# Copying queries and keys into block order on POOL for the two dilated patterns of a hybrid gMLP and attention block

## Chip, cores and metric

The kernel runs on one core of one Trainium2 chip. The metric is the device time of one execution in microseconds (us). Every time below is from that core. The engines are named as in the profile: PE multiplies matrices, PEld loads its stationary operand, DVE, ACT and POOL work element by element, and SP issues nearly all transfers.

## What is computed

One layer on 2048 tokens of width 1024: an input product with a 1024 x 9216 matrix, a gated spatial mixing branch (a), a dilated attention branch (b), gates, two projections and a final norm. The part that the change touches is the attention, with 16 heads of width 64 and three patterns (window, dilation) = (128, 1), (512, 4), (2048, 16). Each pattern takes the tokens by stride and attends within blocks of 128:

```python
def to_blocks(t):
    t = t.reshape(Bn, H, L, dilation, Dh).transpose(0, 1, 3, 2, 4)
    ...
    return t.reshape(Bn, H, dilation, nb, BLOCK, Dh)

qb, kb, vb = to_blocks(q), to_blocks(k), to_blocks(v)
kw, vw = with_prev(kb), with_prev(vb)      # the block before and this one
...
s = jnp.einsum('bhrnqd,bhrnkd->bhrnqk', qb, kw) * (Dh ** -0.5)
s = s - slopes[...] * (dist * dilation)
s = jnp.where(valid, s, NEG_INF)
m = jnp.max(s, axis=-1); p = jnp.exp(s - m[..., None]); l = jnp.sum(p, axis=-1)
o = jnp.einsum('bhrnqk,bhrnkd->bhrnqd', p, vw) / l[..., None]
```

The three results of a head are mixed by their softmax denominators.

## The kernel before

**Stages.** First come normalised inputs and the q, k, v, gate and branch-a products (up to about 1430 us of the profile). Then comes `window`, the attention of all 16 heads, which is interleaved with the remaining dense products, called *fill* (80 products of 24 matmuls each, L116). Last comes `final` (from about 2430 us): the projection of b, the output product and the norm.

**Numbers.** Dense products are exact sums of three products of high and low parts, so every weight block of 1024 x 128 is split on POOL inside the window: `whi` (L85) and then `wlo` (L86). Queries and keys are float16. `Q` holds a head's high and low parts of the queries on its 128 partitions, `KH` and `KL` the high and the low keys, twice each; all three are [128, 2048], tokens in their natural order along the row.

**Attention.** A head has three patterns, taken in the order p = 2 (dilation 16), p = 1 (dilation 4), p = 0 (dilation 1). A pattern has 16 blocks of 128 queries in four groups g. A group goes through three stages, each one step or more behind the other:

- `stage_s`: scores. Per block two matmuls, L407 with `KH` and L408 with `KL`, both with the block's queries of `Q` as the stationary operand, into `ss` in PSUM (two buffers). DVE adds the bias `B` and takes the row maximum (L414, into `S` and `m4`), and L417 scales the four maxima into column 65 of the output tile (`ob` or `OC`). ACT takes the exponential (L422).
- `stage_t`, two steps later: transposes of `S` on PE (L439) into `pt`, then the high part `ph` on ACT (L442) and the low part `pl` on DVE (L443).
- `stage_o`, three steps after the scores: L456 to L458 multiply by `V`, ACT copies the result out (L459).

p = 2 blocks have one block of keys (128 columns). In p = 1 every fourth block has one and the others two (256 columns); in p = 0 only the first has one. Which columns a block reads is said by `cols`:

```python
if p == 0:
    return t[:, P * b:P * (b + n)]
if p == 1:
    return t.rearrange("p (a q) -> p q a", q=4)[:, b // 4, P * (b % 4):P * (b % 4 + n)]
return t.rearrange("p (a q) -> p q a", q=16)[:, b]
```

so that p = 1 reads every 4th float16 (8 bytes apart) and p = 2 every 16th (32 bytes apart).

**Combine.** When p = 0 of a head is done, `combine` runs in pieces during the second half of the next head's p = 2 and its p = 1: small DVE operations (L478 to L488), then four times L497 on DVE (scaling `OC`), L499 on POOL (adding) and L502 on DVE (adding into `cb`). After every second head come four transposes (L509) and L513.

**What sets the order.** PE's order is the program's, since each piece is queued behind the one before (`seg`). The other engines' and SP's queues are filled by a scheduler that takes instructions by priority and by when it reckons them ready; each queue then runs strictly in its order. Tiles that share a tag share its buffers, and an instruction that writes a tile waits until all readers of the buffer's last tile are done.

Of the kernel before, what the change touches and what calls it, by code (L numbers as in the profile page):

```python
# [16 lines left out]
P = 128  # L17
# [10 lines left out]
class Prog:  # L28
# [6 lines left out]
    # ---------------------------------------------------------------- setup  # L35
    def setup(self):
# [15 lines left out]
        # largest |g_norm|, and the scales of q, k (pair of heads) and v (four heads)  # L52
# [21 lines left out]
    # -------------------------------------------------------------- helpers  # L74
# [13 lines left out]
    def wblock(self, wp, w, c0, width, scale=None):  # L88
        """columns c0..c0+width of a weight, as exact high and low parts;
        scale: [P, 1] that gets a scale under which no product with h leaves float16"""  # L90
# [6 lines left out]
        if scale is not None:  # L97
            # |h @ w| <= |h| |w column| <= (32 max|g|) (32 max|w|)
# [40 lines left out]
    # ------------------------------------------------------- normalised input  # L139
# [4 lines left out]
    def split_X(self, X, k, src):  # L144
        """src fp32 -> X[k] exact high and low parts"""
# [29 lines left out]
    def load_X(self, qd, src):  # L175
        X = self.alloc_X(qd % 2)
        for k in range(KC):
            t = self.wk.tile([P, 512], F32, name="xl", tag="xl")
# [15 lines left out]
    def unit_rows(self, wp, X, hf, w, c0, evac, scale=None):  # L194
        """128 tokens on partitions, 256 columns at a time, two such in a bank"""
# [16 lines left out]
    # ---------------------------------------------------------------- q and k  # L212
    def ev_qk(self, dst, s):
        nc = self.nc

        def ev(nb, qd, ps):
            hi = self.wk.tile([P, 512], F16, name="qh", tag="qh")
            lo = self.wk.tile([P, 512], F16, name="ql", tag="ql")
# [36 lines left out]
    # --------------------------------------------------------------- branch a  # L255
# [66 lines left out]
    # ------------------------------------------------------------- gates of b  # L322
# [24 lines left out]
    # -------------------------------------------------------------- attention  # L347
# [28 lines left out]
    def cols(self, t, p, b, n):  # L376
        """n = 1: columns of block b; n = 2: of block b and the next one"""
        if p == 0:
            return t[:, P * b:P * (b + n)]
        if p == 1:  # L380
            return t.rearrange("p (a q) -> p q a", q=4)[:, b // 4, P * (b % 4):P * (b % 4 + n)]
        return t.rearrange("p (a q) -> p q a", q=16)[:, b]

    def stage_s(self, at, G):
        nc = self.nc
        h, p, g = G["h"], G["p"], G["g"]
        Q, KH, KL, B = G["qk"]
# [7 lines left out]
        S = at.tile([P, 4, 256], F32, name="S", tag="S", bufs=4)  # L395
# [3 lines left out]
        for i2 in range(2):  # L399
            ps = self.ps.tile([P, 2, 256], F32, name="ss", tag="ss", bufs=2)  # L400
            for i in range(2):
# [3 lines left out]
                q = self.cols(Q, p, b, 1)  # L405
                w0 = b - 1 if prev else b
                nc.tensor.matmul(ps[:, i, :n], q, self.cols(KH, p, w0, n // P), start=True, stop=False)  # L407
                self.pe = nc.tensor.matmul(ps[:, i, :n], q, self.cols(KL, p, w0, n // P), start=False, stop=True)  # L408
# [360 lines left out]
```

## Time and profile before

| | |
|---|---|
| median of 3 runs | 2826.39 us (2821.72 to 2830.69) |
| span of the profiled execution | 2821.4 us |
| PE busy | 2724.5 us, 97% of the span |
| DVE / ACT / POOL busy | 1195.5 / 1063.8 / 625.6 us |
| first score matmul, last score matmul | 1467.7 us, 2413.8 us |
| score matmuls L407 + L408, busy | 258.5 + 264.7 us (768 each) |

The profiled execution shows no time outside its span; the fastest of the three runs is 0.3 us above the span and their median 5.0 us. Busy time of PE is summed over overlapping matmuls, so what one matmul costs is read from the distance between the starts of consecutive ones, not from its duration. A head starts every 60 us or so.

### The profile page before, as it was taken

The page shows a single profiled execution, that of the slowest core. Times are in us where ns is not written, and L with a number is a line of the kernel's source. Part 1 is how long each engine was busy: PE and PEld are TensorE (multiplying, and loading weights), DVE is VectorE, ACT ScalarE, POOL GpSimd, SP SyncE. Part 2 cuts the span into 40 slices and gives each one's busy share as a digit, 9 for nine tenths or more (in the row PEclk, how much of TensorE's full clock was granted, in tenths as well). Part 3 has the DMA queues.
Part 4 walks back from the last instruction along what each step waited for, and adds up shares of the span by engine and source line. Part 5 has one row for each costly group of instructions (what it writes and reads, how often), then busy time and mean ns, then how long its engine had stood idle before and what let it go on. Part 6 is the DMA issues. An engine that isn't in the chain of part 4 may idle for free.

```text
span 2821.4 us, 44790 instructions
## 1 busy us (share of the span) xinstructions
PE 2724.5 (97%) x17504; PEld 2273.2 (81%) x17504; DVE 1195.5 (42%) x3186; ACT 1063.8 (38%) x2039; POOL 625.6 (22%) x398
## 2 busy tenths in 40 slices
PE   6899899999999999999999999999999999899998
PEld 4779897888887889988877777777777777678887
DVE  6232104331003111013336666677677777555443
ACT  4312212122123222221126666666666666333221
POOL 2322211223233221212231221233333333100000
PEclk9999999999999999999999999999999999999999
DMA  7633402224345333202254556656677676665442
GB/s 230 177 101 85 93 16 76 67 87 134 101 136 155 93 102 84 66 28 68 67 163 115 153 149 169 166 169 182 186 213 221 192 208 187 205 208 183 153 151 74
DMA packets 489332, 381.68 MB, mean 135 GB/s; under 512 B 152224, under 2 KB 414752, under 8 KB 489120
## 3 DMA queue, kind: packets, MB, share of 16 engines
q1 hardware_dynamic: 488688, 378.75, 46.4%
q8 instruction: 137, 2.24, 0.3%
q14 instruction: 75, 0.61, 0.1%
q10 hardware_dynamic: 432, 0.07, 0.0%
HBM read 277.42 MB, written 101.32 MB: 134 GB/s over the span
## 4 chain that ended last, share of the span: by engine, by line
PE 84%; DMA 3%; DVE 3%; ACT 2%; issue 2%; POOL 1%; SPq 0%; DVEq 0%; ACTq 0%; POOLq 0%
PE pj L116 65%; PE ss L407 5%; PE ss L408 5%; PE pt L439 4%; PE po L456 1%; PE po L458 1%; PE po L457 1%; DMA wraw<-in_w_proj_b 1%; PE pt L297 1%; DMA v_d<-vst 1%; ACT junk L281 1%; DVE X L148 1%; PE pt L509 0%; POOL wlo L86 0%; DMA xl<-ya_d 0%
## 5 line engine op out<-in xcount | busy, mean ns | idle before, releaser
L116 PE MATMUL pj<-X,whi 128*128 128x512 f32 x4608 | 1472.0, 398 | 21.4 <-ACT whi L83 8.3
L116 PEld LDWEIGHTS pj<-X,whi 128*128 128x128 f32 x4608 | 868.2, 190 | 202.6 <-ACT whi L83 10.3
L116 PE MATMUL pj<-X,wlo 128*128 128x512 f32 x2304 | 915.5, 397 | 16.1 <-POOL wlo L86 10.8
L86 POOL TENSOR_TENSOR wlo<-wraw,whi 128x1024 fp32r<-128x1024 f32 (+1 forms) x176 | 458.5, 2606 | 763.7 <-ACT whi L83 688.3
L116 PEld LDWEIGHTS pj<-X,wlo 128*128 128x128 f32 x2304 | 437.9, 190 | 109.8 <-POOL wlo L86 12.7
L116 PE MATMUL pj<-whi,X 128*128 128x256 f32 x2048 | 360.7, 279 | 6.9 <-DVE vst L238 6.7
L83 ACT CAST whi<-wraw 128x1024 fp32r<-128x1024 f32 (+1 forms) x152 | 173.2, 1140 | 505.2 <-PE pj L116 445.7
L116 PEld LDWEIGHTS pj<-whi,X 128*128 128x128 f32 x2048 | 312.9, 188 | 8.2 <-issue 7.2
L414 DVE CUSTOM_DVE_ANT_0 S<-ss,B 128x256 f32<-128x256 f32 (+1 forms) x768 | 244.6, 361 | 143.7 <-PE ss L408 142.6
L116 PE MATMUL pj<-wlo,X 128*128 128x256 f32 x1024 | 285.6, 279 | 2.7 <-POOL vst L233 2.7
L422 ACT ACTIVATE S<-S,ob,iqk 128x128 f32<-128x128 f32 (+1 forms) x512 | 231.8, 525 | 95.4 <-DVE ob L417 95.3
L407 PE MATMUL ss<-KH,Q 128*128 128x256 f16 (+1 forms) x768 | 258.5, 356 | 6.9 <-DVE m L414 6.8
L408 PE MATMUL ss<-KL,Q 128*128 128x256 f16 (+1 forms) x768 | 264.7, 358 | 0.0
L443 DVE SCALAR_TENSOR_TENSOR pl<-pt,ph 128x512 f16<-128x512 f32 x320 | 203.4, 653 | 89.8 <-ACT ph L442 88.1
L442 ACT ACTIVATE ph<-pt 128x512 f16<-128x512 f32 x320 | 167.5, 560 | 119.6 <-PE pt L439 119.5
L116 PEld LDWEIGHTS pj<-wlo,X 128*128 128x128 f32 x1024 | 192.6, 188 | 2.9 <-POOL vst L233 2.9
L85 POOL TENSOR_SCALAR whi<-wraw 128x1024 fp32r<-128x1024 f32 x64 | 69.3, 1083 | 539.0 <-PE pj L116 508.6
L116 PE MATMUL pj<-WO,X 128*128 128x512 f32 x768 | 180.1, 395 | 0.9 <-ACT X L632 0.8
L116 PEld LDWEIGHTS pj<-WO,X 128*128 128x128 f32 x768 | 144.1, 188 | 36.2 <-ACT X L632 1.2
L439 PEld LDWEIGHTS pt<-ident,S 128*128 128x128 f32 x1200 | 146.1, 144 | 28.9 <-DVE pl L443 3.6
L439 PE MATMUL pt<-ident,S 128*128 128x128 f32 x1200 | 165.6, 275 | 2.7 <-DVE pl L443 2.7
L422 ACT ACTIVATE S<-S,OC,iqk 128x256 f32<-128x256 f32 (+1 forms) x256 | 131.8, 584 | 52.5 <-DVE OC L417 52.5
(105 smaller groups left out, 2422.5 us busy)
## 6 DMA issues: line engine op xcount, KB each, us to landing
wraw<-in_w_in SPq DMA_DIRECT2D x136, 512.0 KB, 4.1
V<-v_d SPq DMA_DIRECT2D x48, 520.0 KB, 4.2
o_d<-ob SPq DMA_DIRECT2D x32, 528.0 KB, 4.3
OC<-o_d SPq DMA_DIRECT2D x32, 528.0 KB, 5.2
wraw<-in_w_in SPq DMA_DIRECT2D x16, 1024.0 KB, 5.6
wraw<-in_w_proj_a SPq DMA_DIRECT2D x32, 512.0 KB, 5.3
wraw<-in_w_proj_b SPq DMA_DIRECT2D x32, 512.0 KB, 4.5
v_d<-vst SPq DMA_DIRECT2D x128, 65.0 KB, 3.5
```

The source lines that it names most:

```text
L83: nc.scalar.copy(hi, raw)
L85: nc.gpsimd.tensor_scalar(out=hi, in0=raw, scalar1=1.0, scalar2=0.0, op0=ALU.mult, op1=ALU.add)
L86: self.w_lo.tensor_tensor(out=lo, in0=raw, in1=hi.bitcast(F32), op=ALU.subtract)
L116: self.pe = nc.tensor.matmul(out, st(a, k), mv(b, k), start=first and n == 0, stop=last and n == len(todo) - 1)
L148: self.x_lo.tensor_tensor(out=X[k][1], in0=src, in1=X[k][0].bitcast(F32), op=ALU.subtract)
L407: nc.tensor.matmul(ps[:, i, :n], q, self.cols(KH, p, w0, n // P), start=True, stop=False)
L408: self.pe = nc.tensor.matmul(ps[:, i, :n], q, self.cols(KL, p, w0, n // P), start=False, stop=True)
L414: nc.vector.tensor_tensor_reduce(out=S[:, j, :n], in0=ps[:, i, :n], in1=B[:, bo:bo + n], scale=1.0, scalar=-3e38, op0=ALU.add, op1=ALU.max ...
L422: nc.scalar.activation(S[:, i, :rng[i]], S[:, i, :rng[i]], AF.Exp, bias=ob[:, i, 65:66], scale=self.iqk[:, pr:pr + 1])
L439: self.pe = nc.tensor.transpose(px[:, j * P:(j + 1) * P], G["S"][:, i, c * P:(c + 1) * P], self.ident)
L442: nc.scalar.activation(ph[:, :n], px[:, :n], AF.Copy, scale=PSCALE)
L443: nc.vector.scalar_tensor_tensor(out=pl[:, :n], in0=px[:, :n], scalar=PSCALE, in1=ph[:, :n], op0=ALU.mult, op1=ALU.subtract)
```

## The change

`permute` is new: for each head and for p = 2 and p = 1, POOL copies `Q`, `KH` and `KL` into `perm_` tiles in which every block's 128 columns lie next to each other. That is 6 copies of [128, 2048] float16 a head, 96 in all; p = 0 still reads the raw tiles. The scores then read plain slices. The copies for p = 1 of a head are written out after the scores of groups 0, 1 and 2 of its p = 2, and those for p = 2 of the next head after the same groups of p = 0. They use three tags with two buffers each.

Room is made by fewer buffers: `V` 2 for 4, `S` 3 for 4, `ph` and `pl` 3 for 4, and one tag `ld` with 3 buffers in place of `xl` (2) and `gal` (2, used for `gal` and `sbg`). The staging tiles `qh` and `ql` move to a pool of their own that is gone by the time of the window. The load of the next pattern's `V` is written out at group 3 of a pattern and no longer at group 0. Comments are dropped; the PE order is the same, with `perm_` tiles in place of the raw ones.

```diff
-            t = self.wk.tile([P, 512], F32, name="xl", tag="xl")
+            t = self.wk.tile([P, 512], F32, name="xl", tag="ld", bufs=3)
...
-        g = self.wk.tile([P, 512], F32, name="gal", tag="gal")
+        g = self.wk.tile([P, 512], F32, name="gal", tag="ld", bufs=3)
...
-        V = at.tile([P, 16, 130], F16, name="V", tag="V", bufs=4)
+        V = at.tile([P, 16, 130], F16, name="V", tag="V", bufs=2)
...
-    def cols(self, t, p, b, n):
...
+    def permute(self, at, t, p):
+
+        r = at.tile([P, T], F16, name=f"perm_{t.name[:2]}", tag=f"perm{len(self.perm_tags) % 3}", bufs=2)
+        self.perm_tags.append(0)
         if p == 1:
...
+            self.nc.gpsimd.tensor_copy(r.rearrange("p (q n a) -> p q n a", q=4, n=4),
+                                       t.rearrange("p (n a q) -> p q n a", q=4, n=4))
+        else:
+            self.nc.gpsimd.tensor_copy(r.rearrange("p (q a) -> p q a", q=16),
+                                       t.rearrange("p (a q) -> p q a", q=16))
+        return r
...
-        S = at.tile([P, 4, 256], F32, name="S", tag="S", bufs=4)
+        S = at.tile([P, 4, 256], F32, name="S", tag="S", bufs=3)
...
-                q = self.cols(Q, p, b, 1)
-                w0 = b - 1 if prev else b
-                nc.tensor.matmul(ps[:, i, :n], q, self.cols(KH, p, w0, n // P), start=True, stop=False)
-                self.pe = nc.tensor.matmul(ps[:, i, :n], q, self.cols(KL, p, w0, n // P), start=False, stop=True)
+                q = Q[:, P * b:P * b + P]
+                w = slice(P * (b + 1) - n, P * (b + 1))
+                nc.tensor.matmul(ps[:, i, :n], q, KH[:, w], start=True, stop=False)
+                self.pe = nc.tensor.matmul(ps[:, i, :n], q, KL[:, w], start=False, stop=True)
...
-            ph = at.tile([P, 512], F16, name="ph", tag="ph", bufs=4)
-            pl = at.tile([P, 512], F16, name="pl", tag="pl", bufs=4)
+            ph = at.tile([P, 512], F16, name="ph", tag="ph", bufs=3)
+            pl = at.tile([P, 512], F16, name="pl", tag="pl", bufs=3)
...
-        qk[0] = self.load_qk(at, 0)
+        raw = {0: self.load_qk(at, 0)}
+        qk[0, 2] = [self.permute(at, t, 2) for t in raw[0][:3]]
...
+                if g == 3 and j + 1 < n:
+                    q = j // 4 + 1
+                    vt[q // 3, 2 - q % 3] = self.load_v(at, q // 3, 2 - q % 3)
                 if g == 0:
-                    q = j // 4 + 1
-                    if q < 3 * NH:
-                        h2, p2 = q // 3, 2 - q % 3
-                        vt[h2, p2] = self.load_v(at, h2, p2)
...
+                G.update(qk=qk[h, p] if p else raw[h][:3], B=raw[h][3], V=vt[h, p], OC=OC, O=O)
                 run(self.stage_s(at, G))
+
+                nxt = {2: (h, 1), 0: (h + 1, 2)}.get(p)
+                if nxt and nxt[0] < NH and g < 3:
+                    qk.setdefault(nxt, []).append(self.permute(at, raw[nxt[0]][g], nxt[1]))
```

**POOL's queue, around p = 1 of a head in the later half.** The names: `B` is the next head's bias, `OC` the four additions of the combine, `whi` and `wlo` the halves of a fill weight block. Before:

```order
L359 TENSOR_SCALAR B<-B,sqk 128x640
L499 TENSOR_TENSOR OC<-OC 128x4x64 x3
L85 TENSOR_SCALAR whi<-wraw 128x1024
L86 TENSOR_TENSOR wlo<-wraw,whi 128x1024
L499 TENSOR_TENSOR OC<-OC 128x4x64
L85 TENSOR_SCALAR whi<-wraw 128x1024
L86 TENSOR_TENSOR wlo<-wraw,whi 128x1024
```

And now, where L384 is a copy for p = 2 of the next head, L381 one for its p = 1, and L504 the addition that was L499:

```order
L384 COPY perm_KH<-KH 128x2048
L359 TENSOR_SCALAR B<-B,sqk 128x640
L384 COPY perm_Q__19353<-Q 128x2048
L504 TENSOR_TENSOR OC<-OC 128x4x64
L384 COPY perm_KL<-KL 128x2048
L85 TENSOR_SCALAR whi<-wraw 128x1024
L86 TENSOR_TENSOR wlo<-wraw,whi 128x1024
L504 TENSOR_TENSOR OC<-OC 128x4x64 x3
L85 TENSOR_SCALAR whi<-wraw 128x1024
L86 TENSOR_TENSOR wlo<-wraw,whi 128x1024
L381 COPY perm_Q__19667<-Q 128x2048
L381 COPY perm_KH<-KH 128x2048
```

The three copies for p = 2 stand ahead of and among the additions of the combine, and the three for p = 1 follow at once, behind the weight blocks.

**DVE's queue, two groups of p = 0.** `S,m` are the row maxima of L414, `pl` the low part of the transposed probabilities, of which a group has two. Before:

```order
L443 SCALAR_TENSOR_TENSOR pl<-pt,ph 128x512
L417 TENSOR_SCALAR OC<-m_12134,niqk 128x4
L443 SCALAR_TENSOR_TENSOR pl<-pt,ph 128x384
L414 ISA S,m_12205<-ss,B 128x256
L414 ISA m_12205 128x1
L414 ISA S,m_12205<-ss,B 128x256
L414 ISA m_12205 128x1
```

And now, with L448, L422 and L419 for L443, L417 and L414:

```order
L448 SCALAR_TENSOR_TENSOR pl<-pt,ph 128x512
L422 TENSOR_SCALAR OC<-m_12164,niqk 128x4
L419 ISA S,m_12239<-ss,B 128x256
L419 ISA m_12239 128x1
L419 ISA S,m_12239<-ss,B 128x256
L419 ISA m_12239 128x1
L448 SCALAR_TENSOR_TENSOR pl<-pt,ph 128x384
```

The second `pl` of a group, whose buffer is now that of the group before, has moved behind the first half of the next scores.

More of the change, by code (lines that the diff above doesn't have):

```diff
@@ L216, in ev @@
         def ev(nb, qd, ps):
-            hi = self.wk.tile([P, 512], F16, name="qh", tag="qh")
-            lo = self.wk.tile([P, 512], F16, name="ql", tag="ql")
+            hi = self.wq.tile([P, 512], F16, name="qh", tag="qh")
+            lo = self.wq.tile([P, 512], F16, name="ql", tag="ql")
             sc = s[:, nb:nb + 1]
@@ L386, in stage_s @@
         h, p, g = G["h"], G["p"], G["g"]
-        Q, KH, KL, B = G["qk"]
+        Q, KH, KL = G["qk"]
+        B = G["B"]
         period = (16, 4, 1)[p]
@@ L509, in combine @@
                 self.pe = nc.tensor.transpose(px[:, r * P:(r + 1) * P], cb[:, 4 * g + r], self.ident)
-            sb = self.wk.tile([P, 512], F32, name="sbg", tag="gal")
+            sb = self.wk.tile([P, 512], F32, name="sbg", tag="ld", bufs=3)
             nc.sync.dma_start(out=sb, in_=self.bg_d[g][i * P:(i + 1) * P])
@@ L525, in window @@
         qk, vt = {}, {}
+        self.perm_tags = []
         att_total = (0.109 * 2 + 0.088) * 75 * NH + 8 * 4 * 0.45
@@ L558, in window @@
                     if p == 1 and h + 1 < NH:
-                        qk[h + 1] = self.load_qk(at, h + 1)
+                        raw[h + 1] = self.load_qk(at, h + 1)
                 if g == 0:
                     O = OC[:, 0] if p == 0 else at.tile([P, 16, 66], F32, name="ob", tag="ob", bufs=2)
-                G.update(qk=qk[h], V=vt[h, p], OC=OC, O=O)
+                G.update(qk=qk[h, p] if p else raw[h][:3], B=raw[h][3], V=vt[h, p], OC=OC, O=O)
                 run(self.stage_s(at, G))
+                nxt = {2: (h, 1), 0: (h + 1, 2)}.get(p)
+                if nxt and nxt[0] < NH and g < 3:
+                    qk.setdefault(nxt, []).append(self.permute(at, raw[nxt[0]][g], nxt[1]))
             if 2 <= j < n + 2:
@@ L663, in load_Y @@
         for k in ks:
-            t = self.wk.tile([P, 512], F32, name="xl", tag="xl")
+            t = self.wk.tile([P, 512], F32, name="xl", tag="ld", bufs=3)
             self.nc.sync.dma_start(out=t, in_=self.yb_d[qd][k * P:(k + 1) * P])
@@ L679, in run @@
             hp = s1.enter_context(tc.tile_pool(name="hp", bufs=2))
+            self.wq = s1.enter_context(tc.tile_pool(name="wq", bufs=2))
             X = [None, None]
```

4 lines of the change are left out of this document (removed).

## Prediction

> **What bounds the kernel now.** I read the page's busy shares first, then the window of the attention by stretches, then the single matmuls in the timeline, then who waited for whom.
>
> ```profile
> PE 2724.5 (97%) x17504; PEld 2273.2 (81%) x17504; DVE 1195.5 (42%) x3186; ACT 1063.8 (38%) x2039; POOL 625.6 (22%) x398
> ```
>
> PE looks like the bound, but its busy time is modelled. The timeline's starts say more. Columns: start, duration, engine, line, operation. First p = 2 (128 columns, 32 bytes apart), then p = 1 (128 and 256 columns, 8 bytes apart), then p = 0 (dense):
>
> ```profile
> 1700.89 0.42 PE L407 MATMUL ss<-KH,Q 128*128 128x128 f16 x1
> ...
> 1702.56 0.41 PE L408 MATMUL ss<-KL,Q 128*128 128x128 f16 x1
> ...
> 1715.81 0.28 PE L407 MATMUL ss<-KH,Q 128*128 128x128 f16 x1
> ...
> 1716.03 0.41 PE L407 MATMUL ss<-KH,Q 128*128 128x256 f16 x1
> ...
> 1717.18 0.41 PE L408 MATMUL ss<-KL,Q 128*128 128x256 f16 x1
> ...
> 1733.85 0.22 PE L407 MATMUL ss<-KH,Q 128*128 128x128 f16 x1
> ...
> 1733.96 0.27 PE L407 MATMUL ss<-KH,Q 128*128 128x256 f16 x1
> ...
> 1740.17 0.28 PE L407 MATMUL ss<-KH,Q 128*128 128x256 f16 x1
> ...
> 1740.94 0.27 PE L408 MATMUL ss<-KL,Q 128*128 128x256 f16 x1
> ```
>
> Distance over count: p = 2, 1.67 us over 7 steps, 0.239 us a matmul; p = 1, 0.22 over 2 = 0.110 (128 columns) and 1.15 over 5 = 0.230 (256); p = 0, 0.11 over 2 = 0.055 (128) and 0.77 over 7 = 0.110 (256). The same shapes cost 4.3 and 2.1 times the dense price when their columns lie apart.
>
> Now the stretches of one early and one late head, each cut at the first scores of p = 2, p = 1 and p = 0. Columns: stretch, length, busy us of PE, PEld, DVE, ACT and POOL, granted clock, DMA share, GB/s.
>
> ```profile
> 1519.60:1540.00 20.40, 20.40 (x179) 16.09 (x176) 10.87 (x52) 11.74 (x31) 4.23 (x3) 1.00 0.77 201
> 1540.00:1558.10 18.10, 18.10 (x150) 13.60 (x147) 16.22 (x53) 11.14 (x26) 6.52 (x6) 1.00 0.15 46
> 1558.10:1576.50 18.40, 18.40 (x189) 15.70 (x186) 11.68 (x45) 14.44 (x32) 0.58 (x1) 1.00 0.59 157
> ...
> 1934.50:1954.80 20.30, 20.30 (x177) 15.98 (x174) 9.92 (x51) 12.79 (x32) 6.98 (x5) 1.00 0.73 180
> 1954.80:1972.80 18.00, 18.00 (x148) 13.36 (x145) 16.91 (x51) 11.95 (x28) 7.73 (x6) 1.00 0.57 176
> 1972.80:1995.00 22.20, 22.20 (x215) 19.07 (x212) 13.67 (x48) 14.15 (x31) 6.89 (x4) 1.00 0.67 191
> ```
>
> PE is full in all three and the clock is 1.00. But in p = 1, where the combine runs, DVE is busy 16.2 to 16.9 of 18 us: PE bounds it by little. In p = 2 and p = 0 DVE has room. PE's own waits over the window are small, and all but one group name DVE:
>
> ```profile
> PE ss L407 <- DVE m L414: 6.8, 6, 2.4
> PE po L456 <- ACT ob L459: 3.1, 3, 1.1
> PE pt L439 <- DVE pl L443: 2.7, 2, 2.5
> PE po L458 <- DVE pl L443: 1.3, 1, 1.3
> ```
>
> Where the longest comes from matters most for this change. Rows of POOL, DVE and PE around 2155 us:
>
> ```profile
> 2151.38 2.39 POOL L86 TENSOR_TENSOR wlo<-wraw,whi 128x1024 fp32r<-128x1024 f32 x1
> ...
> 2152.15 1.64 DVE L417 TENSOR_SCALAR ob<-m,niqk 128x4 f32<-128x4 f32 x1
> ...
> 2158.40 0.22 PE L407 MATMUL ss<-KH,Q 128*128 128x128 f16 x1 [2.36 <-DVE m L414]
> ```
>
> L417 writes four numbers a partition. Here it takes 1.64 us and ends at 2153.79, 0.02 us after POOL's L86 (2153.77). The same pairing stands at 1919.96:
>
> ```profile
> 1919.58 2.69 POOL L86 TENSOR_TENSOR wlo<-wraw,whi 128x1024 fp32r<-128x1024 f32 x1
> ...
> 1919.96 2.35 DVE L417 TENSOR_SCALAR OC<-m,niqk 128x4 f32<-128x4 f32 x1
> ...
> 1925.68 0.55 PE L439 MATMUL pt<-ident,S 128*128 128x128 f32 x3 [2.47 <-DVE pl L443]
> ```
>
> Undisturbed, L417 takes 0.22 us (next rows). So some DVE operations stand still until POOL's running instruction ends, and PE then waits 2.4 us. Operations that read PSUM do not; L148 (0.68 us alone, 1.53 beside an L85), the combine's L483 to L502 and L417 do.
>
> ```profile
> 1918.50 1.53 DVE L148 TENSOR_TENSOR X<-xl,X 128x512 fp32r<-128x512 f32 x1 [0.67 <-ACT X L147]
> ...
> 1998.81 0.22 DVE L417 TENSOR_SCALAR ob<-m,niqk 128x4 f32<-128x4 f32 x1
> 1998.94 0.69 DVE L443 SCALAR_TENSOR_TENSOR pl<-pt,ph 128x512 f16<-128x512 f32 x1
> ...
> 2033.98 0.68 DVE L148 TENSOR_TENSOR X<-xl,X 128x512 fp32r<-128x512 f32 x1
> ```
>
> **The change part by part.**
>
> *Dense scores, PE.* Per head, p = 2 has 32 matmuls of 128 columns: 32 x (0.239 - 0.055) = 5.9 us. p = 1 has 24 of 256 and 8 of 128: 24 x (0.230 - 0.110) + 8 x (0.110 - 0.055) = 3.3 us. That is 9.2 us a head, 147 us for 16. PE's order is unchanged, so this is on the path as long as the others keep up: p = 2 would go from 20.3 to 14.4 us, p = 1 from 18.0 to 14.7.
>
> *The copies, POOL.* No copy of this kind stands in the trace. The nearest rows have one operand and are dense:
>
> ```profile
> L85 POOL TENSOR_SCALAR whi<-wraw 128x1024 fp32r<-128x1024 f32 x56 | 60.9, 1087 | 492.8 <-PE pj L116 473.8 <-DVE pl L443 16.5 <-DMA wraw<-in_w_proj_a 2.4
> ...
> L499 POOL TENSOR_TENSOR OC<-OC 128x256 f32<-128x256 f32 x60 | 49.0, 821 | 115.7 <-DVE ob L417 32.7 <-DVE OC L497 29.5 <-ACT ph L442 23.1
> L359 POOL TENSOR_SCALAR B<-B,sqk 128x640 f32<-128x640 f32 x14 | 12.1, 863 | 51.4 <-DMA B<-in_bias 51.4
> ```
>
> 2048 elements at L85's rate are 2.1 us, the lower bound for both kinds. Upper bounds scale it by what PE pays for the stride: 2.1 x 2.1 = 4.4 us (p = 1) and 2.1 x 4.3 = 9.1 us (p = 2). For the value I take PE's cost per strided column as the rate at which such columns come out of memory: 0.230/256 = 0.90 ns (8 bytes), below POOL's own 1.06 ns, so p = 1 stays at 2.1 us; 0.239/128 = 1.87 ns (32 bytes), 2048 of them 3.8 us, with a start 4.0 us for p = 2. A head's POOL work in the late part is then five weight blocks at 1.09 + 2.4, four L499, one L359 and 3 x (2.1 + 4.0): about 40 us of 55 to 60. POOL is not the bound by sum.
>
> *The copies' effect on DVE.* The p = 2 copies write buffers that the last p = 2 scores of the head before free, so they run at the end of p = 2 and in p = 1, where DVE is fullest. I walk that stretch by hand, t = 0 at that release, first p = 1 scores due at 3.6. `KH` copy 0 to 4.0: DVE does two L414 and stands in L483 from 0.4 (3.6 us lost). L359 4.0 to 4.8; `Q` copy to 8.8: DVE gets through L484 and stands in L485 (3.7 lost). The third waits for L499, which waits for L497, so it runs about 11.6 to 15.6 and holds L417 for some 2 us. Together 9.3 us. p = 1 then needs 16.6 of DVE (mean of the two heads) + 9.3; one group, 3.7 us, can be carried into p = 0, since `ss` has two buffers. 22.2 us instead of 18.0. In p = 0 the three 2.1 us copies cost about 1.4 each (DVE has one 0.69 us L443 or so to do before it stands), with the 3.7 carried 13.7 + 4.2 + 3.7 = 21.6 of 22.2 late, 19.6 of 18.4 early: +0.5 on the mean. p = 2 keeps its 14.4, DVE at 10 to 12.
>
> *The sum.* 15 heads x (-5.9 + 4.2 + 0.5) = -18; the last head makes no copies for a next one, -9.2. Together -27 from 2821.4: 2794, and with the median 5 above the profiled span, 2799 us.
>
> *Fewer buffers.* `S` with 3: L414 of group j reuses the buffer whose transposes (group j-3) PE has done just ahead of these scores; nothing. `ph`/`pl` with 3: the second pair waits until L456 to L458 of the group before have read; it is used a group, 4 us, later, and DVE's queue has L414 moved ahead of it, so the cover is that group; without it, the 0.7 us of one `pl` a group. `V` with 2: the load waits on SP for L458 of two patterns ago, now right behind, and is needed four groups (17 us) later against 4.2 us to landing; what is queued behind it (`wraw`, `o_d`) waits under a group:
>
> ```profile
> V<-v_d SPq DMA_DIRECT2D x48, 520.0 KB, 4.2
> ```
>
> `ld`: `gal`, `sbg` and `xl` share three buffers; a transfer of 5 us against 12 us a product; `xl` in the last phase gets one more. I cost all at 0 to 5 us and take 0.
>
> *Start.* The first scores need three copies (12 us) after their loads; six products of fill, 144 matmuls, stand ahead. 0, at worst 5.
>
> **The rivals.**
>
> *Cheap copies.* POOL may not mind the stride: 2.1 us for all. Each copy in p = 1 then blocks 1.9 us less: 45 x 1.9 = 86 more, 2713 us. For it: POOL's rate is half of PE's per column. Against: 32 bytes cost PE fourfold.
>
> *A half surcharge.* POOL may pay a fixed part for the stride; midway between 2.1 and 4.0 the p = 2 copy is 3.1 us, 45 x 0.9 = 40 more, 2759 us. [...] No row here shows a strided POOL read.
>
> *Slower.* Every further us of the p = 2 copy stands in DVE's way in p = 1, 45 us in all. The gain is gone at 4.0 + 27/45 = 4.6 us; at 5.5 us the kernel takes 2867, and at 9.1 over 3000. For it: 1.87 ns is only what PE's readers reach, and each copy is one more chance to hold L483 to L502. Against: nothing shows POOL reading slower than PE.
>
> *Even.* Copies at 4.4 to 4.8 us, or DVE losing 2 us more a head than in my walk: within 9 us of now.
>
> *Late copies.* PE waits for `perm_` tiles: for p = 2 they end in p = 1 and are due a whole p = 0 (22 us) later; I give it nothing of its own.
>
> *No dense price.* Then p = 0's rows would not be half of p = 1's; excluded.
>
> **How the numbers follow.** Forecast (copies of 3.5 to 4.4 us) 0.35, its own range 2777 to 2816; half surcharge 0.12; cheap 0.17; even 0.11; slower 0.25. A change under 0.3%, 8.5 us, can't be told from none. Faster 0.35 + 0.12 + 0.17 = 0.64, same 0.11, slower 0.25. The range goes from 2712 (cheap copies) to 2867 (5.5 us), leaving out under 0.1 on each side.
>
> **What would show it.** Starts of L412/L413 in p = 2 at 0.055 apart and p = 1 at 0.110: the PE term. L384 and L381 at 4.0 and 2.1 us: the price. L417's successor L422, L483 and L502 ending with the copies and PE waiting for `m` and `pl` in p = 1, which takes 22 us: the loss. p = 2 stretches of 14.4 us. I am wrong if PE stays full in p = 1 (DVE gets through between the copies), if a copy is far from 4 us, or if PE waits for `perm_` or `V`.

## The result, and the profile after

The changed kernel takes 2927.5 us (2924.8 to 2931.5), the kernel before 2826.7 beside it: the ratio is 1.0359, 95% interval 1.034 to 1.0378. It is slower by 101 us where 27 less were forecast.

The page's line of busy shares: PE loses its full share, DVE and POOL gain time.

```profile
PE 2650.7 (90%) x17504; PEld 2245.4 (77%) x17504; DVE 1395.7 (48%) x3186; ACT 1058.4 (36%) x2039; POOL 911.7 (31%) x494
```

The first and last of the eight score matmuls of a p = 2 group (timeline: start, duration, engine, line). 0.39 us over 7 steps is 0.056 us each, where it was 0.239:

```profile
2253.74 0.22 PE L412 MATMUL ss<-perm_KH,perm_Q__21240 128*128 128x128 f16 x1
...
2254.13 0.22 PE L413 MATMUL ss<-perm_KL,perm_Q__21240 128*128 128x128 f16 x1
```

POOL's groups in the window of the attention, the copies for p = 2 (L384) and for p = 1 (L381). The last column is idle time before them. They cost 4.0 and 2.1 us, as forecast:

```profile
L384 POOL COPY perm_KL<-KL 128x2048 f16<-128x2048 f16 x15 | 60.6, 4040 | 0.0
L384 POOL COPY perm_KH<-KH 128x2048 f16<-128x2048 f16 x15 | 60.4, 4028 | 46.0 <-PE ss L413 46.0
...
L381 POOL COPY perm_KL<-KL 128x2048 f16<-128x2048 f16 x16 | 34.3, 2144 | 0.0
L381 POOL COPY perm_KH<-KH 128x2048 f16<-128x2048 f16 x16 | 33.1, 2069 | 9.0 <-PE ss L412 8.8
```

The stretches of a late head, p = 2, p = 1, p = 0 (columns as in the prediction: stretch, length, busy us of PE, PEld, DVE, ACT, POOL, granted clock, DMA share, GB/s):

```profile
2253.70:2268.20 14.50, 14.50 (x177) 12.49 (x174) 9.97 (x43) 10.46 (x26) 7.02 (x6) 1.00 0.98 251
2268.20:2295.80 27.60, 18.54 (x149) 15.10 (x146) 27.53 (x61) 11.12 (x25) 21.34 (x12) 0.81 0.31 88
2295.80:2321.50 25.70, 23.07 (x218) 19.18 (x215) 17.25 (x50) 14.41 (x32) 10.04 (x6) 1.00 0.70 202
```

p = 2 is 14.5 us here, as forecast (14.4). p = 1 is 27.6 instead of 22.2, DVE is busy in all of it (an operation that is held counts as busy), PE in two thirds, and PE's granted clock is 0.81. p = 0 is 25.7, though DVE is busy in only 17 of them. What happens at the start of that p = 1 (timeline; in brackets the idle time before and who ended it):

```profile
2268.19 3.87 POOL L384 COPY perm_Q__22129<-Q 128x2048 f16<-128x2048 f16 x1
...
2268.48 3.62 DVE L489 TENSOR_TENSOR mn<-lw 128x16 f32<-128x16 f32 x1
2272.01 3.92 POOL L384 COPY perm_KH<-KH 128x2048 f16<-128x2048 f16 x1
2272.23 3.73 DVE L490 TENSOR_TENSOR mn<-mn,lw 128x16 f32<-128x16 f32 x1
2272.36 0.28 PE L412 MATMUL ss<-perm_KH,perm_Q__21554 128*128 128x256 f16 x1 [3.59 <-DVE m L419]
...
2275.87 3.91 POOL L384 COPY perm_KL<-KL 128x2048 f16<-128x2048 f16 x1
2276.64 3.17 DVE L422 TENSOR_SCALAR ob<-m,niqk 128x4 f32<-128x4 f32 x1
...
2279.85 1.65 ACT L427 ACTIVATE S<-S,ob,iqk 128x128 f32<-128x128 f32 x4 [11.92 <-DVE ob L422]
...
2281.40 0.35 ACT L464 COPY ob<-po 128x260 f32<-128x260 f32 x1
2281.80 0.21 PE L461 MATMUL po<-V,ph 128*128 128x65 f16 x1 [4.95 <-ACT ob L464]
```

Each of these three copies holds one DVE operation to its end, as forecast. Over the window 43 of the 45 copies for p = 2 do so, and 32 of the 47 for p = 1. What the forecast missed is what follows. L422 comes late, behind two held operations and held itself, so ACT stands 11.92 us at its exponential; L464, which has nothing to do with this group's scores, is queued behind that exponential on ACT, and PE waits 4.95 us for it. Over the window the waits of PE of these four kinds grew from 14 us to 179 (line waited for: us, times, longest):

```profile
PE po L463 <- DVE pl L448: 62.1, 28, 7.4
PE po L461 <- ACT ob L464: 47.8, 32, 6.6
PE ss L412 <- DVE m L419: 43.5, 37, 6.7
PE pt L444 <- DVE pl L448: 25.2, 21, 3.8
```

None names `perm_` or `V`. From 1467 to 2500 us DVE never waits for POOL's results, and PE does so for 4.3 us (`whi` and `wlo`).

### The profile page after: what moved, and what is told of

Same layout as the page of the kernel before. It is cut to its first block, busy times and chain, and to the rows that moved or that the text cites. A ratio compares the mean times of both kernels' runs of the same rounds, so it can differ in the third digit from the quotient of the medians.

```text
span 2929.8 us, 44970 instructions
## 1 busy us (share of the span) xinstructions
PE 2650.7 (90%) x17504; PEld 2245.4 (77%) x17504; DVE 1395.7 (48%) x3186; ACT 1058.4 (36%) x2039; POOL 911.7 (31%) x494
## 4 chain that ended last, share of the span: by engine, by line
PE 59%; DVE 20%; DMA 6%; ACT 6%; issue 3%; POOL 1%; SPq 0%; DVEq 0%; POOLq 0%; ACTq 0%
PE pj L116 53%; DVE S L419 4%; DVE ob L422 3%; ACT S L427 3%; DVE pl L448 3%; DVE cb L507 2%; DVE OC L502 2%; PE pt L444 1%; DVE X L148 1%; DMA wraw<-in_w_out 1%; DVE mn L490 1%; PE pt L297 1%; DMA wraw<-in_w_in 1%; ACT ph L447 1%; DMA o_d<-ob 1%
## 5 line engine op out<-in xcount | busy, mean ns | idle before, releaser
L116 PE MATMUL pj<-X,wlo 128*128 128x512 f32 x2304 | 923.3, 401 | 23.4 <-POOL wlo L86 12.3
L448 DVE SCALAR_TENSOR_TENSOR pl<-pt,ph 128x512 f16<-128x512 f32 x320 | 205.2, 652 | 110.5 <-ACT ph L447 108.6
L419 DVE CUSTOM_DVE_ANT_0 S<-ss,B 128x256 f32<-128x256 f32 (+1 forms) x768 | 239.2, 358 | 35.2 <-PE ss L413 34.9
L444 PE MATMUL pt<-ident,S 128*128 128x128 f32 x1200 | 177.3, 284 | 26.0 <-DVE pl L448 25.2
L463 PE MATMUL po<-V,pl 128*128 128x65 f16 x1200 | 136.0, 197 | 62.3 <-DVE pl L448 62.1
L461 PE MATMUL po<-V,ph 128*128 128x65 f16 x1200 | 138.1, 196 | 56.0 <-ACT ob L464 47.8
```

The costliest lines, as they stand in the source:

```text
L116: self.pe = nc.tensor.matmul(out, st(a, k), mv(b, k), start=first and n == 0, stop=last and n == len(todo) - 1)
L419: nc.vector.tensor_tensor_reduce(out=S[:, j, :n], in0=ps[:, i, :n], in1=B[:, bo:bo + n], scale=1.0, scalar=-3e38, op0=ALU.add, op1=ALU.max ...
L444: self.pe = nc.tensor.transpose(px[:, j * P:(j + 1) * P], G["S"][:, i, c * P:(c + 1) * P], self.ident)
L448: nc.vector.scalar_tensor_tensor(out=pl[:, :n], in0=px[:, :n], scalar=PSCALE, in1=ph[:, :n], op0=ALU.mult, op1=ALU.subtract)
L461: nc.tensor.matmul(o, ph[:, sl], V[:, kb, 64:129], start=first, stop=False)
L463: self.pe = nc.tensor.matmul(o, pl[:, sl], V[:, kb, 64:129], start=False, stop=last)
```

## The experiments

Three theories stood against each other. Theory 1: POOL's copies hold DVE, and PE waits for what comes late. Theory 2: the fewer buffers make the waits. Theory 3: POOL's queue is late with its other work behind the copies. The 4.3 us above speak against the third in the changed kernel.

Two quantities are worked out from the traces. **Stretches** are means over heads 1 to 14, from the first score matmul of a pattern to that of the next. **Held time** is the sum over DVE's instructions from 1467 to 2540 us of what each takes beyond the lower quartile that its line and shape has in the kernel with dense slices and no copies; an excess below 0.05 us is not counted. All experiments start from the changed kernel; the line numbers shift with the edits.

| kernel | us | p = 2, p = 1, p = 0 | held us |
|---|---|---|---|
| before | 2824 | 20.3, 18.4, 21.2 | 48 |
| dense, no copies | 2750 | 15.8, 18.0, 21.3 | 70 |
| plain copies | 2837 | 16.1, 21.3, 23.4 | 167 |
| scaling on ACT | 2893 | 15.9, 26.9, 22.1 | 212 |
| copies moved | 2918 | 16.0, 22.7, 27.1 | 243 |
| after | 2928 | 16.5, 26.8, 24.1 | 263 |
| copies in eighths | 2923 | 16.2, 26.2, 22.5 | 163 |
| eighths, sum on DVE | 2885 | 16.2, 24.0, 22.4 | 184 |
| copies on ACT | 2874 | 15.7, 24.5, 22.0 | 60 |
| copies for p = 1 alone | 2822 | 20.5, 18.0, 21.3 | 105 |
| copies for p = 2 alone | 2862 | 20.4, 21.3, 20.6 | 163 |

The same can be read by stretch. Against the kernel with dense slices and no copies, DVE is held in the changed kernel 1.3, 9.5 and 2.8 us a head more in p = 2, p = 1 and p = 0, and these stretches are 0.6, 8.8 and 2.7 us longer.

**The buffers alone.** Scores read strided columns as before, no copies, the change's buffer counts.

```diff
-qk=qk[h, p] if p else raw[h][:3]
+qk=raw[h][:3]            # and cols() as before
```

> This kernel keeps the re-shared buffers of the change (ph and pl 3, V 2, S 3, ld 3 shared) but has no copies on POOL: the scores read strided columns as before. Theory 1 (DVE stands still behind the copies): nothing left that holds DVE, so the time is that of before, 2826 us within 8. Rival 2 (the smaller buffers make the new waits for pl, ob and S): the waits stay, 2880 to 2930 us.

Measured: 2824.4 us, ratio 0.9999 (0.9989 to 1.0009). The buffers cost nothing at this pace. Theory 2 falls for strided scores; with dense ones the same buffers are tried again below.

**PE's gain alone.**

```diff
-qk=qk[h, p] if p else raw[h][:3]
+qk=raw[h][:3]            # dense slices of the loaded tiles
```

> The scores of the two dilated patterns read dense columns of the loaded tiles; the reordering is left out, so those two patterns see other tokens than they should. What is left is TensorE's gain alone. By the prediction's PE term (9.2 us a head, 147 us): 2826 - 147 = 2680 us. If PE was not the limit in those stretches (DVE or ACT close behind it), less comes out: 2720 us or more. Rival 2 (smaller buffers cost 50 to 100 us): 2730 to 2780 us.

Measured: 2749.6 us, ratio 0.9731 (0.9706 to 0.9756): 74 us of the 147. A late head by stretches, and PE's largest wait:

```profile
2117.80:2132.40 14.60, 14.60 (x180) 12.60 (x177) 10.08 (x44) 10.46 (x26) 7.09 (x5) 1.00 1.05 256
2132.40:2151.30 18.90, 16.78 (x149) 13.49 (x146) 16.82 (x62) 12.76 (x29) 6.39 (x6) 0.91 0.48 135
```

```profile
PE ss L412 <- DVE m L419: 22.5, 24, 4.3
```

p = 1 stays at 18 to 19 us though PE has matmuls for less. So the copies, from 2750 to 2928, cost 178 us.

**Shorter instructions.**

```diff
-gpsimd.tensor_copy(r as (q a), t as (a q))
+for i in range(8): gpsimd.tensor_copy(one eighth of the columns)
```

> Each copy of POOL is cut into 8 instructions, each for an eighth of the columns, one after the other; POOL's total work is the same (12 us a head for p=2, 6.3 for p=1) with some more fixed cost. Theory 1 (a DVE operation on SBUF waits until the POOL instruction that runs has ended, one DVE operation for each POOL instruction): a wait of up to 0.5 us takes the place of one of up to 4.0 us; of the 158 us by which the copies hold DVE some 30 to 60 are left, PE's waits shrink with them, 2740 to 2830 us. Rival 3 (POOL's queue is late with whi, wlo and the products of combine behind the copies): the same or slower, 2927 to 2950 us. Rival 2 (buffers): 2927 us.

Measured: 2922.7 us, ratio 1.0355 (1.0327 to 1.0384). A miss for theory 1. The held time did fall, from 263 to 163 us, but the time hardly did. The first two rows are POOL's groups, the third is from DVE's timeline:

```profile
L388 POOL COPY perm_KL<-KL 128x256 f16<-128x256 f16 x127 | 90.8, 760 | 0.0
...
L384 POOL COPY perm_KL<-KL 128x256 f16<-128x256 f16 x128 | 48.9, 440 | 0.0
```

```profile
2277.24 0.83 DVE L510 TENSOR_TENSOR cb<-OC 128x256 f32<-128x256 f32 x1 [4.76 <-POOL OC L507]
```

An eighth takes 0.76 us where 4.04/8 is 0.51, and the sum of the products (L507) stands behind 24 such pieces in POOL's queue. DVE waits for it in order, 62 us in all, with the row maxima behind it. So part of the holds was exchanged for a wait: of the 173 us over the kernel without copies, 93 are held time and up to 62 this wait.

**Eighths, and that sum on DVE.**

```diff
-nc.gpsimd.tensor_add(OC[:, 0, r, :HD], ...)
+nc.vector.tensor_add(OC[:, 0, r, :HD], ...)
```

> The copies in eighths as before, and the sum of the first two patterns' products (L504) on DVE instead of POOL, so that DVE no longer waits in order for a sum that stands behind 24 pieces of copy in POOL's queue (62 us of DVE's waits in the kernel with eighths). DVE gets 64 additions of about 0.4 us more (26 us). If that wait took the place of the lock: 2923 - 62 + 26 or better, 2830 to 2890 us. If eighths hold DVE as much as whole copies do by something else: 2915 us or more.

Measured: 2885.0 us, ratio 1.0222 (1.0202 to 1.0242): 38 us better, so the wait was a good part of it. It is at the slow end of what was expected. The sum itself is now held, as its row in DVE's groups shows, where an undisturbed sum of this shape takes 0.41 us:

```profile
L507 DVE TENSOR_TENSOR OC<-OC 128x256 f32<-128x256 f32 x64 | 47.3, 741 | 0.0
```

135 us remain over the kernel without copies. 114 us more held time and 26 of added work on DVE, together 140, account for them.

**One heavily held operation off DVE.**

```diff
-nc.vector.tensor_scalar(out=ob[:, :, 65], in0=m4, scalar1=niqk, op0=mult)
+nc.scalar.activation(ob[:, :, 65], m4, Copy, scale=niqk)
```

> The scaling of the four row maxima (L422, one DVE tensor_scalar on 4 columns for each group, the operation that is held most) is issued on ScalarE instead; the copies stay as they are. Theory 1 with the handover as I read it (a held L422 holds the exponentials behind it on ACT, these the transposes and PE): the 100 us of L422's excess go and most of PE's wait for ob with them, 2830 to 2880 us; combine's operations (L489, L490, L502, L507, some 100 us) are still held and pl behind them. If the waits of PE come from those and not by way of L422: 2910 to 2927 us. Rivals 2 and 3: 2927 us.

Measured: 2893.2 us, ratio 1.0243 (1.0222 to 1.0263), 34 us better than the changed kernel, between the two expectations. PE no longer waits for `ob` through L422 (13 us instead of 55), but for `pl`, and longer for `m` (59 us for 43.5):

```profile
PE po L462 <- DVE pl L447: 76.2, 25, 7.6
```

The held time falls only to 212 us, 51 less, though L422 alone has 101 us of the 263 in the changed kernel: other operations are held about 50 us longer. Some of the 34 us need not be the holds: the same move is worth 19 us in a kernel without copies (the last section of the experiments).

**The copies on ScalarE.**

```diff
-self.nc.gpsimd.tensor_copy(
+self.nc.scalar.copy(
```

> The six copies of a head run on ScalarE instead of POOL; everything else is that of the changed kernel. DVE is no longer held by copies, POOL is as free as before, but ACT gets the copies between its exponentials. Theory 1 (holds of DVE by POOL): DVE's excess falls back to 50 to 70 us as without copies; if an ACT copy takes about 2 us, ACT gains 12 us a head on its 40 to 43 of 55, gets full, and the time is 2790 to 2860 us, with PE waiting for ACT now. If instead the loss comes from when the copies are made (their data, their buffers): 2920 us.

Measured: 2873.6 us, ratio 1.0178 (1.0161 to 1.0194); DVE's held time is 60 us. That lies above the first expectation and below the second. The holds are gone, and ACT is the bound in p = 1 (busy in 24.0 of 24.5 us, means over heads 1 to 14), since a p = 2 copy takes it as long as POOL, not the 2 us supposed:

```profile
L384 ACT COPY perm_KL<-KL 128x2048 f16<-128x2048 f16 x15 | 61.4, 4094 | 0.0
...
L381 ACT COPY perm_KL<-KL 128x2048 f16<-128x2048 f16 x16 | 33.6, 2099 | 0.0
```

```profile
PE po L461 <- ACT ob L464: 77.5, 36, 4.5
```

**Copies without reordering.**

```diff
-gpsimd.tensor_copy(r as (q a), t as (a q))
+gpsimd.tensor_copy(r, t)
```

> POOL copies all six tiles without reordering them (dense in, dense out); the dense slices of p=1 and p=2 then see other tokens than they should, the reordering being left out. Each copy lasts what a dense one does. By the prediction's slope (45 us of time for each us of a p=2 copy) with copies of 2.1 us: 2927 - 1.9 x 45 = 2842 us, 2830 to 2855. If a dense copy is much shorter (1 us): 2780 to 2810. If what matters is that three instructions stand in POOL's queue, not their length: 2900 us or more.

Measured: 2836.9 us, ratio 1.0052 (1.0035 to 1.0068), inside the first expectation. The copies take 1.9 to 2.0 us for p = 2 (L383) as for p = 1 (L381):

```profile
L381 POOL COPY perm_KL<-KL 128x2048 f16<-128x2048 f16 x15 | 30.2, 2015 | 0.0
L383 POOL COPY perm_KL<-KL 128x2048 f16<-128x2048 f16 x15 | 29.9, 1996 | 0.0
```

4.04 - 2.00 = 2.04 us less on 45 copies is 92 us; the time fell by 91. The prediction's slope holds here: a us less of a p = 2 copy is about a us less of the kernel.

**Copies moved.** The copies for p = 2 get the buffers that p = 1's scores read last, and so start later.

```diff
-tag=f"perm{i % 3}", bufs=2
+tag=f"perm{i % 3}_{(i // 3 + 1) // 2 % 2}", bufs=1
```

> The same copies on POOL, in the same number of buffers, but a p=2 copy for the next head writes the buffer that this head's p=1 scores read, so it can only start once these are through: the 12 us of p=2 copies move out of the p=1 stretch, where DVE is full with the combine, into p=0, where it is busy 12 to 14 of 18 to 22 us. Theory 1 with DVE's fullness in p=1 as the reason why nothing absorbs the holds: p=1 falls from 26 to 17 or 18 us, p=0 grows by 0 to 3 us over its 24, 2790 to 2850 us. If the sum of the holds counts wherever they lie: 2910 to 2930 us. If the copies are now late for p=2: PE waits for perm, above 2930 us.

Measured: 2917.8 us, ratio 1.0338 (1.031 to 1.0367). A miss: my theory that only p=1, where DVE is full, cannot absorb them, falls. Of the 12.3 us of p = 2 copies a head, 8.8 now lie in p = 0 and 3.5 in p = 1 (before the move 9.9 of 12.0 lay in p = 1). The copies for p = 1 moved too: 4.7 us of them a head lie in p = 1, where it was 2.4. A late head, p = 1 and p = 0:

```profile
2261.50:2283.10 21.60, 16.58 (x149) 13.50 (x146) 21.53 (x60) 11.17 (x25) 15.78 (x10) 0.92 0.39 115
2283.10:2311.70 28.60, 24.03 (x215) 20.09 (x212) 20.15 (x51) 14.40 (x32) 16.01 (x7) 0.94 0.63 182
```

p = 1 gained 4.1 us a head and p = 0 lost 3.0, though DVE is idle for 8.5 of these 28.6 us. The held time moved alike: 4.0 us a head less in p = 1 and 2.8 more in p = 0. DVE's idle time by sum is no room for a hold.

**One part alone.** Copies made and read for one pattern, the other strided.

```diff
-if nxt and nxt[0] < NH and g < 3:
+if nxt and nxt[0] < NH and g < 3 and nxt[1] == 1:     # and == 2
```

> Only the copies for p=1 are made and read; p=2 reads strided columns of the loaded tiles as before. PE gains 3.3 us a head by spacing, of which p=1's full DVE lets through about 1; DVE is held by copies of 2.1 us, some 40 us in all by the changed kernel's trace. If holds pass into the time one for one: 2824 - 15 + 40 to 60 = 2850 to 2870 us. If those in p=0 and p=2 are absorbed: 2800 to 2825 us.

> Only the copies for p=2 are made and read; p=1 reads strided columns as before. PE gains up to 5.9 us a head in p=2 (4.4 by the kernel with dense slices, 70 us), DVE is held by the copies of 4.0 us in p=1, 121 us in the changed kernel's trace. One for one: 2824 - 70 + 121 = 2875 us, 2855 to 2890. If p=1, strided and so 18 us of PE, absorbs part: 2800 to 2850 us. The two parts together should make about the 103 us of the whole change if they add.

Measured: 2822.4 us, ratio 0.9998 (0.9986 to 1.001), for p = 1, and 2861.5, ratio 1.014 (1.0119 to 1.0162), for p = 2. The first is inside the expectation of absorption (2800 to 2825 us), the second inside that of one for one (2855 to 2890); together some 37 us and not 101. Both sets find a free buffer early here and run mostly in p = 2 (5.6 of 6.2 and 10.6 of 12.1 us a head). With strided p = 2 scores (first row) PE stays full beside 12.6 us of POOL; with dense ones (second row) the stretch needs 25.5 us:

```profile
2170.90:2191.20 20.30, 20.30 (x176) 15.60 (x173) 14.22 (x46) 10.93 (x26) 12.59 (x8) 1.00 0.81 211
```

```profile
2201.00:2226.50 25.50, 17.46 (x178) 14.67 (x174) 21.97 (x50) 10.50 (x26) 18.81 (x8) 0.87 0.61 153
```

By the means, the first kernel's p = 2 holds DVE 2.2 us a head more than with the buffers alone and is 0.15 us longer (20.45 for 20.30). The second's is held 5.4 us more than with dense slices and is 4.6 longer. So holds of 2 us beside a slow PE are absorbed, holds of 4 us beside a fast one are not. The length by itself does not decide: the plain copies above hold 2 us each, beside dense scores, and are not absorbed.

**What took the other half of PE's gain.** The combine's products and first sum are left out in the first of these; the buffers of before are given back in the second.

```diff
-nc.vector.tensor_mul(OC, OC, w); nc.gpsimd.tensor_add(OC[0], OC[0], OC[1])
+pass
```

```diff
-V 2, S 3, ph 3, pl 3
+V 4, S 4, ph 4, pl 4
```

> The kernel with dense slices and no copies (the reordering is left out), and the combine's products with the weights and the first sum (L502, L504) are left out as well. They are 4.1 us of DVE a head, in p=1. In the kernel with dense slices PE gained 74 us instead of 147. If DVE's fullness in p=1 is what took the rest: p=1 falls from about 17.3 to 15 us and p=2 to 14.5, 2690 to 2720 us. If ACT or the lower granted clock took it: 2740 us or more.

> Dense slices of the loaded tiles, no copies (the reordering is left out), and V 4, S 4, ph and pl 4 as before. If the fewer buffers cost at the new pace what they cost in the kernel with one order of keys (2790 to 2760): 2715 to 2730 us. If the fewer buffers cost nothing here, DVE's fullness being what counts: 2745 to 2755 us, as with the fewer buffers (2750).

Measured: 2721.5 us, ratio 0.9643 (0.9623 to 0.9663), with p = 1 at 16.1 us; and 2741.0, ratio 0.9704 (0.9689 to 0.9719). The first lies just above its first expectation, the second between its two. DVE's work in the combine takes 28 us, and the buffers 9 by the medians, whose intervals overlap. Some 36 of the missing 73 us stay unexplained. Without the combine's products p = 2 takes 16.6 us and not 14.4, p = 1 16.1 and not 14.7.

**Layouts without copies.** Four kernels let stage 1 write the keys in an order that the scores can read in runs.

```diff
 # first two: a second order beside the natural one
+a as (r a) = hi as (a r), r = 16;  KH, KL loaded in both orders
 # third: only (t mod 16, t div 16);  fourth: only (t mod 4, t div 4)
+keys of a block permuted: bias columns and V's rows permuted to match
```

> No copies in the attention at all: stage 1, where the engines besides TensorE are idle for the most part, writes the keys a second time with the tokens of each 512 in the order (t mod 16, t div 16), and the loads bring both orders. The scores read runs of 128, 32 or 32 keys; queries are read strided, as the stationary operand, from one order. The keys of p=1 stand permuted within a block, with bias and V permuted to match. POOL does nothing more than before. If a strided stationary operand costs little (at most 0.11 us for 128 columns): 2755 to 2790 us, near the kernel without copies (2750). If it costs what strided moving columns cost: p=2 stays at 0.24 us a matmul, 2800 us or more.

> As the kernel with the second order of keys written in stage 1, mended in the two places where its trace lost time: the second order is now copied from SBUF (ACT the high parts, DVE the low ones), so PSUM is free sooner (57 us were lost ahead of the first scores), and the natural keys, which only p=0 reads, are loaded by themselves when their head begins, so that the transfers do not come all at once (PE waited 47 us for weight parts there). If these two were the loss: 2755 to 2785 us, faster than the kernel before. If the further 1 MB of keys a head is what costs, however it is spread: 2815 us or more.

> No copies and no second order: stage 1 writes the keys of each 512 tokens once, in the order (t mod 16, t div 16). All three patterns read that one order: p=2 in runs of 32 keys, p=1 in runs of 32, p=0 in runs of 8 (16 bytes); where p=1 and p=0 see the keys of a block permuted, bias and V are permuted to match. Queries stay in natural order. Transfers are those of the kernel before but for V, which comes in 16 pieces for p=0 and 4 for p=1. If runs of 16 bytes are read at the dense price, and nothing is lost in stage 1: 2750 to 2775 us, near the kernel with dense slices. If such short runs cost p=0 as strided columns did (0.2 us for 128): 2800 to 2830 us. If the pieces of V hold up the transfers behind them: 2790 us or more, with PE waiting for weight parts.

> One order of keys again, now (t mod 4, t div 4) within each 512 tokens: p=1 reads runs of 128, p=0 runs of 32 (keys of a block permuted, bias and V to match), p=2 every fourth key, 8 bytes apart, 0.110 us for 128 columns. V comes in 4 pieces for p=0 and whole for the others, so SP issues 3 transfers more a head instead of 18 (0.4 us each). No copies. PE has 0.055 x 32 = 1.8 us a head less gain than with dense p=2, but p=2 came out at 16 us anyway in the kernel with dense slices: 2750 to 2785 us, faster than before. If three more pieces still make weights late: 2800 us or more.

Measured: 2842.5 (1.0065, 1.0045 to 1.0085), 2838.9 (1.0054, 1.0038 to 1.007), 2905.9 (1.0281, 1.0259 to 1.0304) and 2809.0 us (0.9957, 0.994 to 0.9974). p = 2 now takes 0.063 us a matmul, in the fourth 0.121 (medians of the spacings); three lose more elsewhere. All four are slower than their first expectation. With the second order the first scores come 57 and 64 us later than before, so the mending did not help; PE's waits in stage 1 name `ql`, `whi` and `wlo` there, and what makes these late is open. In the third, V comes in 16 pieces, and SP needs 6.93 us to issue 15 of them (second row, SP's timeline), the weights behind them:

```profile
PE pj L116 <- POOL whi L85: 91.2, 14, 16.3
```

```profile
2052.88 6.93 SPq L375 DMA_DIRECT2D V<-v_d  x15
```

With 4 pieces that wait is 31 us, and the kernel is a little faster than before.

**The version that beats both.** The last layout, with the scaling on ACT, and then with the buffers of before.

```diff
+nc.scalar.activation(ob[:, :, 65], m4, Copy, scale=niqk)
+V 4, S 4, ph 4, pl 4                                     # second run
```

> The kernel with one order (t mod 4) and the scaling of the row maxima (L422) on ScalarE instead of DVE: 2.6 us a head less DVE (192 operations of 0.22 us), about as much more ACT. If DVE's fullness in p=1 still sets the time: 10 to 25 us below that kernel. If ACT is as near its limit: the same or up to 10 us slower.

> The kernel with one order (t mod 4) and the scaling on ScalarE, with the buffers of before (V 4, S 4, ph and pl 4), for which there is room without copies. If the loads of V, waiting on SP for a buffer, hold up the weights behind them: 2760 to 2780 us. If the number of transfers and not their waiting makes the weights late: 2785 to 2795 us, the same as with fewer buffers.

Measured: 2789.8 us, ratio 0.9892 (0.9873 to 0.9911), then 2759.8, ratio 0.9782 (0.9769 to 0.9796). The scaling is worth 19 us even where no copy holds it. The buffers, which cost nothing at the old pace, are worth 30 here: PE's wait for `whi` falls to 18 us (29.5 with fewer buffers), that for `wlo` to 8 (17.5), and SP's waits for a buffer of V (89 us) are no longer among its largest.

```profile
PE 2625.3 (95%) x17600; PEld 2250.2 (82%) x17600; DVE 1151.9 (42%) x2994; ACT 1105.8 (40%) x2231; POOL 622.6 (23%) x398
```

```profile
PE pj L116 <- POOL whi L85: 18.1, 3, 10.0
```

A late head there, p = 2 and p = 1, with PE's clock at 1.00. Over heads 1 to 14 the means are 16.8 and 18.0 us, and in p = 1 the clock's mean is 0.95:

```profile
2116.30:2132.80 16.50, 16.50 (x177) 14.53 (x174) 10.37 (x44) 10.74 (x28) 7.01 (x5) 1.00 0.87 203
2132.80:2149.00 16.20, 15.01 (x149) 12.55 (x145) 15.62 (x55) 14.29 (x35) 6.47 (x6) 1.00 0.45 150
```

## Why the prediction was wrong

**The misses add up.** Forecast were p = 2 14.4, p = 1 22.2 and p = 0 +0.5 us a head. Measured are 16.5, 26.8 and +2.9. The differences, 2.1 + 4.6 + 2.4 = 9.1 us on some 14 or 15 heads, are 127 to 137 us; the miss is 2927.5 - 2799 = 128. It has two parts. Without the copies' holds the walk in the prediction gives p = 2 14.4 and p = 1 16.6, a gain of 15 x 7.3 + 9.2 = 119 us, and 74 came. With them it adds 6.1 us a head, 92, and 178 came.

**Right: the copies' price,** 4.0 and 2.1 us, and with it the falls of the cheap and the half-surcharge rival. A step of 32 bytes cost POOL twice the dense copy (4.04 against 2.00 us), a step of 8 bytes 6% more (2.14 against 2.02).

**Right: the hold.** Forecast 9.3 + 4.2 = 13.5 us a head; measured (263 - 70) / 15 = 12.9. Beside the copies for p = 2 it is 9.1 (forecast 9.3), beside those for p = 1 3.0 (forecast 4.2). The rows show it as one DVE operation for each copy: L490 takes 3.73 us and L422 3.17 (0.22 undisturbed), both ending 0.03 us after a copy that had started before them. L419 and L448, which read PSUM, are not held: their longest take 0.43 and 0.69 us, their medians are 0.41 and 0.68. No run shows why the ones are held and the others not.

**Wrong: "one group, 3.7 us, can be carried into p=0", and "+0.5 on the mean" there.** Of 13.5 us of holds I let 6.1 reach the end (22.2 - 16.6 in p = 1 and 0.5 in p = 0). The runs show nearly all of it, 11.9 us a head (178 / 15): between the kernel without copies and four with whole copies on POOL the time grows by 0.90, 1.01, 0.97 and 0.92 us for each us of held time (plain 87 over 97, scaling on ACT 144 over 142, moved 168 over 173, after 178 over 193; the second is taken against a base without the move to ACT). I compared DVE's busy sum with the stretch's length, as if DVE could make up its delay there. It cannot. In p = 1 it is busy, holds included, in 26.6 of 26.8 us (means over heads 1 to 14). In p = 0 it is busy in 17.5 of 24.1, and yet that stretch grows by its holds: each group passes in order through L422, the exponential, the transposes, `pl` and `ob`, with other groups' work queued behind on ACT and DVE; the 11.92 and 4.95 us in the rows above are this. Moving most of the p = 2 copies into a stretch where DVE idles for 8.5 us changed 10 us of 178. The one case of absorption is that of short copies beside a strided p = 2.

**Wrong: PE's term of 147 us.** The spacings are as forecast, but 74 us came out. In the kernel without copies 3.3 us a head are missing in p = 1 (18.0 for 14.7) and 1.4 in p = 2 (15.8 for 14.4). In that p = 1 DVE is busy in 17.4 of 18.0 us; the prediction let it pass in 16.6, the busy time of two heads of the kernel before. Lightening the combine shows 28 us of this to be DVE's; the buffers take at most some 9, and the rest is open.

**Buffers at 0:** right at the pace of before and, within 9 us, for the dense kernel; in the fastest version they are worth 30 us.

**The rivals.** The slower one named the right side with the wrong cause: copies above 4.6 us. The even one came nearer with its second condition, DVE losing 2 us more a head than in my walk. DVE was not held more than forecast (12.9 for 13.5), but about 6 us a head more of it reached the end (11.9 - 6.1). Late copies did not occur.

**The lower clock** (0.81 in the p = 1 shown, 0.87 to 0.94 in others with gaps, 1.00 in the head shown of the fastest version) appears only in stretches where PE stood idle, though not in all of these (the p = 0 of the result has 2.6 us without PE at 1.00). In p = 1 PE is busy for 17.8 us at a mean clock of 0.84, in the kernel without copies for 15.8 at 0.97. So it may add to the loss; no run took it by itself.

## What to carry to other kernels

Work given to an idle engine is priced by what it holds elsewhere: here each us for which POOL's copies held DVE cost about a us of the kernel (0.90 to 1.01 in four kernels), in p = 1 and in p = 0, and only short copies (2.1 us) beside the slow strided p = 2 were free (ratio 0.9998). When a stretch is walked by hand, follow the delayed item through every queue it passes and not the sums of busy time; two engines with idle time can still form one chain, as in the p = 0 shown, where ACT is busy for 14.4 and DVE for 17.3 of 25.7 us. All four kernels that write the keys in a readable order at first beat the one that reorders them later; only the one that adds few transfers, and no second order of keys, to the queue that also brings the weights beat the kernel before.

## What the hardware showed beside this

- The strided read costs POOL and ACT the same: 2048 float16 at 32 bytes' distance 4.04 and 4.09 us, at 8 bytes 2.14 and 2.10 (the `KL` rows).
- PE read runs of 16 bytes at the dense price: in the third layout p = 0, in runs of 8 keys, kept its 0.056 us for 128 columns (median of the spacings). A p = 2 matmul of 128 columns, keys in runs of 32, whose stationary operand has 32 bytes between its columns, took 0.063.
- SP takes 0.3 to 0.6 us to issue a transfer (medians by line, before and after), a sixteenth of V in the third layout (0.29, L375) not much less than a whole one there (0.38, L381); 15 small pieces are 6.93 us of its queue.
